# A two-layer decoder step on one core: the stores of the first FFN phase go to GpSimd, and the loads of the samples and of the residual are tied to their step

## The chip, the cores and the metric

The kernel runs on one core of a Trainium2 chip. The metric is the device time of one execution in microseconds (us); of several executions the median counts. A core has five engines that run side by side, each through its own list of instructions in order: TensorE (PE, matrix products, with its weight loads shown apart as PEld), VectorE (DVE), ScalarE (ACT), GpSimd (POOL) and SyncE (SP). Any of SP, ACT and GpSimd can issue a DMA; an engine that has to wait before it may issue one also holds up everything behind it in its list.

## The reference

Two decoder layers over 1024 prompt rows and 8 samples of 8 rows each (1088 rows, width 1024), in float32. The change touches the second half of a layer, the gated FFN with a causal convolution of width 3 (5632 channels in, 2816 after the gate):

```python
h = _rmsnorm(x, p['g_ffn']) * (1 + sc_f) + sh_f
hu = h @ p['w_ffn_in']
ext = jnp.concatenate([conv_prev.astype(hu.dtype), hu], axis=1)
conv = p['conv_b'] + sum(p['conv_w'][j] * ext[:, j:j + t] for j in range(CONV_W))
gate, up = jnp.split(conv, 2, axis=-1)
x = x + g_f * ((jax.nn.silu(gate) * up) @ p['w_ffn_out'])
return x, k, v, vg, ext[:, -(CONV_W - 1):]
```

For the prompt `conv_prev` is zero; each sample brings two rows of its own. The last two rows of `ext` are an output too.

## The kernel before

Every float32 product is made of three products of a high and a low part (high x high, high x low, low x high). ACT rounds a tile to its high part and DVE subtracts to get the low part (`split`, L181 and L182).

The first FFN phase computes `hu` in 22 blocks f of 128 gate and 128 up channels, from seven products each (L916). Behind a block, `conv(f, i)` stores the 64 sample columns of `hu` to a scratch tensor `hsd` (L936, 32 KB) and its last two prompt columns to the output (L937, 1 KB), and makes the convolution of the prompt columns on ACT and DVE. `gate(f)` multiplies the two halves on DVE (L950) and stores the gated product to the scratch tensor `pd[f]` (L951, 512 KB). A layer has 44 + 44 + 22 = 110 such stores, and SP issues them between the loads of the weights.

The second FFN phase multiplies by `w_ffn_out`. `down(g)` is a pass over 22 steps f for one third of the 1088 columns (t = g // 2: 384, 384 and 320 columns) and one half of the output rows (mh = g % 2), g = 0 to 5. A step makes 12 matmuls (L304, L305, L306 for four PSUM banks). It needs the weight `ro`, split to `oh` and `ol` (`half_unit`, L1058: three raw buffers, six of each split part), and in passes with mh = 0 the product `pr` loaded from `pd` and split to `ph` (`load_prod`, L1052: three raw buffers; 25 split ones, so the next pass uses them again). Tile names carry layer, f, then mh and t: `ro1_1710` is layer 1, f = 17, mh = 1, t = 0, and `pr1_130` is layer 1, f = 13, t = 0.

`samples()` is called in the text at g = 1, f = 10. It loads the samples' rows `hs` from `hsd` (L1068, 1408 KB) and their old rows `hal` (L1071), copies both into `ext` (L1075 on ACT, L1074 on GpSimd), saves the new last rows (L1077, L1079), makes the convolution with six large DVE operations (L1090, L1091, and L1093, L1094 twice; tiles `sa` and `sm`), SiLU on ACT (L1096), the gate on DVE (L1097), and 22 stores of `sa` into the sample columns of `pd` (L1099, 32 KB each), which only the passes g = 4 and 5 read. At f = 8 of each pass `hook` loads the four residual tiles `xb` that the end of the pass needs (L1129); there L293 adds the products to the residual and L1118 or L1120 stores it.

In what order an engine runs all this is not set by the text alone: a scheduler places each instruction in its engine's list, as early as its buffers, its data and its own reckoning of time allow, so a load can go far ahead of the place where it is written. `after(a, b)` (L88) keeps instruction a behind instruction b in that placing, without a wait on the chip. The kernel uses it elsewhere already.

Of the kernel before, what the change touches and what calls it, by code (L numbers as in the profile page):

```python
# [16 lines left out]
P = 128  # L17
D = 1024
KD = D // P
NP = 1024  # L20
NSEQ = 8
DT = 8
# [5 lines left out]
NF = DFF // P  # L28
# [19 lines left out]
def hybrid_decoder_kernel(  # L48
# [5 lines left out]
    nc = tc.nc  # L54
# [15 lines left out]
    def big(shape, dt, nm):  # L70
        q = "bb" if nm.startswith(late) else "ba"
        return pl[q].tile(shape, dt, tag="b", name=nm, bufs=9)
# [4 lines left out]
    def bank(tag, nm):  # L77
        return pl["ps"].tile([P, 512], F32, tag=tag, name=nm, bufs=4)
# [9 lines left out]
    def after(inst, prev):  # L88
        tc.add_manual_dep(
            inst.ins, prev.ins.name,  # L90
            mybir.DependencyInfo(mybir.DependencyClass.NoSync, mybir.DependencyReason.DATA),
            reason="issue order")
# [64 lines left out]
    def unit(l, u, eng=nc.vector):  # L157
        wp = pl["wp"]
        raw = wp.tile([P, 1024], F32, tag="raw", name=f"r{l}_{u}", bufs=NRAW)
        nc.sync.dma_start(out=raw, in_=w[l, u])  # L160
        wh = wp.tile([P, 1024], F32R, tag="wh", name=f"wh{l}_{u}", bufs=6)
        wl = wp.tile([P, 1024], F32R, tag="wl", name=f"wl{l}_{u}", bufs=6)
        nc.scalar.activation(out=wh, in_=raw, func=AF.Copy)  # L163
        eng.tensor_tensor(out=wl, in0=raw, in1=wh.bitcast(F32), op=ALU.subtract)  # L164
        return wh, wl
# [136 lines left out]
    def mm3(pt, lh, ll, rh, rl, first, last):  # L302

        r = nc.tensor.matmul(pt, lhsT=lh, rhs=rh, start=first, stop=False)  # L304
        nc.tensor.matmul(pt, lhsT=lh, rhs=rl, start=False, stop=False)  # L305
        nc.tensor.matmul(pt, lhsT=ll, rhs=rh, start=False, stop=last)  # L306
        return r
# [97 lines left out]
    xs = [big([P, T], F32, f"x0_{m}") for m in range(KD)]  # L405
# [106 lines left out]
    for l in range(DEPTH):  # L512
# [10 lines left out]
        for g in range(4):  # L523
            wh, wl = unit(l, U_ZU + g)
            pts = [bank(tags[g % 2], f"zu{l}_{g}{t}") for t in range(3)]
# [255 lines left out]
        xo = dp.tile([KD, P, T], F32, tag=f"xo{l}", name=f"xo{l}")  # L781
# [4 lines left out]
        xs = []  # L786
# [141 lines left out]
        pd = [dp.tile([P, T], F32, tag=f"pd{l}_{f}", name=f"pd{l}_{f}") for f in range(NF)]  # L928
        hsd = dp.tile([P, NCH, NS], F32, tag=f"hsd{l}", name=f"hsd{l}")
        hus, cvs, xps = {}, {}, {}  # L930

        def conv(f, i, to=bp):

            ch = i * NF + f
            hu = hus.pop((f, i))
            nc.sync.dma_start(out=hsd[:, ch], in_=hu[:, NP:])  # L936
            nc.sync.dma_start(out=o_cp[l, :, ch], in_=hu[:, NP - 2:NP])  # L937
            a = cvs[f, i] = to(f"cv{l}_{f}{i}")
            w0, w1, w2 = (L[:, L_CW + j * NCH + ch:L_CW + j * NCH + ch + 1] for j in range(3))
            cb = L[:, L_CB + ch:L_CB + ch + 1]  # L940
            nc.scalar.activation(out=a[:, :NP], in_=hu[:, :NP], func=AF.Identity, scale=w2, bias=cb)  # L941
            for sh, wt in ((1, w1), (2, w0)):
                nc.vector.scalar_tensor_tensor(out=a[:, sh:NP], in0=hu[:, :NP - sh], scalar=wt,  # L943
                                               in1=a[:, sh:NP], op0=ALU.mult, op1=ALU.add)
            if i == 0:
                nc.scalar.activation(out=a[:, :NP], in_=a[:, :NP], func=AF.Silu)  # L946

        def gate(f):
            g, u = cvs.pop((f, 0))[:, :NP], cvs.pop((f, 1))[:, :NP]
            nc.vector.tensor_tensor(out=u, in0=g, in1=u, op=ALU.mult)  # L950
            nc.sync.dma_start(out=pd[f][:, :NP], in_=u)  # L951

        def tail(f):
            prod(xps[f], "T4", "A22", False, True)
# [31 lines left out]
        for i in range(2):  # L986
            conv(0, i, lambda nm: first[1][:, i])
# [55 lines left out]
        xs = []  # L1043
        for m in range(KD):
            xs.append(pl["xb"].tile([P, T], F32, tag=f"x{m}", name=f"xb{l}m{m}", bufs=1))
        acc = {"of": lambda nm: pl["xb"].tile([P, T], F32, tag="acc", name=nm, bufs=1)}
        prods = {}

        def load_prod(f, t):
            o, n = THIRDS[t]  # L1050
# [13 lines left out]
        def samples():  # L1064

            sc = pl["sc"]
            hs = sc.tile([P, NCH * NSEQ, DT], F32, tag="hs", name=f"hs{l}", bufs=1)
            nc.sync.dma_start(out=hs, in_=hsd.rearrange("p c (s i) -> p (c s) i", i=DT))  # L1068
            hal = sc.tile([P, NCH * NSEQ, 2], F32, tag="hal", name=f"hal{l}", bufs=1)
            for i in range(2):  # L1070
                nc.sync.dma_start(out=hal[:, i * NF * NSEQ:(i + 1) * NF * NSEQ],  # L1071
                                  in_=halo[l, i].rearrange("p f s j -> p (f s) j"))
            ext = sc.tile([P, NCH * NSEQ, 2 + DT], F32, tag="ext", name=f"ext{l}", bufs=1)
            nc.gpsimd.tensor_copy(ext[:, :, :2], hal)  # L1074
            nc.scalar.activation(out=ext[:, :, 2:], in_=hs, func=AF.Copy)  # L1075
            new = sc.tile([P, NCH * NSEQ, 2], F32, tag="new", name=f"new{l}", bufs=1)
            nc.gpsimd.tensor_copy(new, ext[:, :, DT:])  # L1077
            for i in range(2):
                nc.sync.dma_start(out=o_cs[l, i].rearrange("p f s j -> p (f s) j"),  # L1079
                                  in_=new[:, i * NF * NSEQ:(i + 1) * NF * NSEQ])  # L1080
            a = sc.tile([P, NCH, NSEQ, DT], F32, tag="a", name=f"sa{l}", bufs=1)
            tm = sc.tile([P, NCH, NSEQ, DT], F32, tag="hs", name=f"sm{l}", bufs=1)

            def rows(j):
                return ext[:, :, j:j + DT].rearrange("p (c s) i -> p c s i", s=NSEQ)

            def per(o):
                return L[:, o:o + NCH].unsqueeze(2).unsqueeze(3).to_broadcast([P, NCH, NSEQ, DT])

            nc.vector.tensor_tensor(out=a, in0=rows(2), in1=per(L_CW + 2 * NCH), op=ALU.mult)  # L1090
            nc.vector.tensor_tensor(out=a, in0=a, in1=per(L_CB), op=ALU.add)  # L1091
            for j in (1, 0):
                nc.vector.tensor_tensor(out=tm, in0=rows(j), in1=per(L_CW + j * NCH), op=ALU.mult)  # L1093
                nc.vector.tensor_tensor(out=a, in0=a, in1=tm, op=ALU.add)  # L1094
            af = a.rearrange("p c s i -> p c (s i)")
            nc.scalar.activation(out=af[:, :NF], in_=af[:, :NF], func=AF.Silu)  # L1096
            nc.vector.tensor_tensor(out=af[:, NF:], in0=af[:, :NF], in1=af[:, NF:], op=ALU.mult)  # L1097
            for f in range(NF):
                nc.sync.dma_start(out=pd[f][:, NP:], in_=af[:, NF + f])  # L1099

        def down(g, hook):
            t, mh = divmod(g, 2)
            o, n = THIRDS[t]
            pts = [bank(tags[g % 2], f"y{l}_{g}{i}") for i in range(4)]
            for f in range(NF):
                wh, wl = half_unit(f, mh, t)
                if mh == 0:
                    load_prod(f, t)
                for i in range(4):
                    mm3(pts[i][:, :n], wh[:, i * P:(i + 1) * P], wl[:, i * P:(i + 1) * P], prods[f][:, 0, :n],  # L1110
                        prods[f][:, 1, :n], f == 0, f == NF - 1)
                hook(f)
            for i in range(4):
                m = 4 * mh + i
                residual(l, t, xs[m], pts[i], 5, m, f"y{l}{g}")
                if l + 1 < DEPTH:
                    square_sum(acc, xs[m], t, m, f"n{l}")
                    nc.sync.dma_start(out=xd[m, :, o:o + n], in_=xs[m][:, o:o + n])  # L1118
                else:
                    nc.sync.dma_start(out=y[m, :, o:o + n], in_=xs[m][:, o:o + n])  # L1120
# [4 lines left out]
        def hook(f):  # L1125
            if f == 8:
                o, n = THIRDS[g // 2]
                for m in range(4 * (g % 2), 4 * (g % 2) + 4):
                    nc.sync.dma_start(out=xs[m][:, o:o + n], in_=xo[m, :, o:o + n])  # L1129
            if g == 1 and f == 10:  # L1130
                samples()
            if l + 1 < DEPTH:
                if g in (2, 4):
                    if g == 2 and f == 0:
                        A1[0] = norm_scale(l + 1, L_GA, 1, f"a{l + 1}")
                    if f == 2:
                        hht, gen[0] = norm(l + 1, g // 2 - 1, xs, acc, A1[0], 0, f"a{l + 1}")
                        h.append(hht)
                    elif f > 2:
                        advance(gen[0], 1)  # L1140
                if g in (1, 3) and 1 <= f <= 8:
                    ada_tag[0] = "mm"
                    ada(1, 1)
                    ada_tag[0] = "at"
# [162 lines left out]
```

## Time and profile before

| | |
|---|---|
| median of 3 runs | 2339.3 us (2336.26 to 2341.22) |
| profiled execution | 2337.34 us, of which its span 2335.5 |
| TensorE's clock, mean | 0.988 of full speed |
| busy: PE, DVE, ACT, GpSimd | 2257.0, 1568.4, 1070.2, 93.6 us |

The span runs from the first to the last instruction of one profiled execution. Busy time does not count the issuing of DMAs. An engine that is idle off the chain of work that ends last costs nothing. TensorE's clock has two levels, 2.4 GHz (1.00 in the table by stretch) and 1.2 GHz (0.50); a stretch with both shows a value between them.

### The profile page before, as it was taken

Reading aid. Unit: us, or ns where it says so; the run is one execution under the profiler, and the core shown is the slowest. Engines: PE = TensorE matmul, PEld = TensorE weight load, DVE = VectorE, ACT = ScalarE, POOL = GpSimd, SP = SyncE. Lnnn points to the kernel's source line nnn. Section 1 sums busy time; section 2 is a strip of 40 time slices with the busy share of each in tenths; the row PEclk is TensorE's granted clock in tenths of the full one; section 3 lists DMA queues with packets and bytes.
Section 4 is the critical chain, followed back from the end, with each engine's and each line's share of the span. In section 5 each row is a group of like instructions: output and inputs, shape, how many; then the busy total and the mean of one; then the engine's idle time right before and its main releaser. Section 6 shows DMA issues by size and latency. Waiting matters only on the chain.

```text
span 2335.5 us, 40665 instructions
## 1 busy us (share of the span) xinstructions
PE 2257.0 (97%) x15838; PEld 2127.7 (91%) x15838; DVE 1568.4 (67%) x3238; ACT 1070.2 (46%) x2026; POOL 93.6 (4%) x78
## 2 busy tenths in 40 slices
PE   7999999999999998999999999989999999969999
PEld 5898789899999998899989977789999999969999
DVE  6837845987777777574667488269777777675543
ACT  5525534644444444354544355246444444444442
POOL 1000002000000000000100000110000000000000
PEclk9999999999999999999999999999999999989999
DMA  9220244322222226867441002741222222187653
GB/s 350 101 89 1 75 165 163 123 81 85 77 82 79 76 68 224 276 212 246 155 156 48 32 1 96 247 139 48 85 77 76 77 84 78 57 262 239 202 186 131
DMA packets 163489, 294.78 MB, mean 126 GB/s; under 512 B 47200, under 2 KB 88800, under 8 KB 163040
## 3 DMA queue, kind: packets, MB, share of 16 engines
q1 hardware_dynamic: 163296, 292.18, 37.5%
q8 instruction: 124, 2.03, 0.3%
q14 instruction: 69, 0.57, 0.1%
HBM read 245.42 MB, written 46.69 MB: 125 GB/s over the span
## 4 chain that ended last, share of the span: by engine, by line
PE 88%; DVE 4%; DMA 3%; ACT 2%; issue 1%; SPq 1%; POOL 0%; DVEq 0%; ACTq 0%; POOLq 0%
PE X L916 23%; PE Y L916 11%; PE o L313 7%; PE y L306 7%; PE y L304 7%; PE y L305 7%; PE Z L916 6%; PE zu L313 4%; PE s L644 2%; PE ada L130 1%; PE av L732 1%; PE q L304 1%; PE zv L306 1%; PE zv L305 1%; PE q L305 1%; PE zv L304 1%
## 5 line engine op out<-in xcount | busy, mean ns | idle before, releaser
L304 PE MATMUL y<-ph,oh 128*128 128x384 f32 (+1 forms) x1056 | 347.9, 331 | 24.2 <-ACT oh L181 18.6
L305 PE MATMUL y<-ph,oh 128*128 128x384 f32 (+1 forms) x1056 | 348.3, 330 | 2.8 <-DVE ph L182 2.8
L306 PE MATMUL y<-ph,ol 128*128 128x384 f32 (+1 forms) x1056 | 347.4, 329 | 0.9 <-DVE ol L182 0.9
L182 DVE TENSOR_TENSOR ol<-ro,oh 128x512 fp32r<-128x512 f32 x264 | 183.3, 702 | 188.5 <-ACT oh L181 177.1
L181 ACT ACTIVATE oh<-ro 128x512 fp32r<-128x512 f32 x264 | 165.8, 630 | 256.0 <-DMA ro<-in_w 123.8
L943 DVE SCALAR_TENSOR_TENSOR cv<-hu,lc,cv 128x1023 f32<-128x1023 f32 (+1 forms) x168 | 215.3, 1282 | 48.2 <-ACT cv L941 46.6
L304 PEld LDWEIGHTS y<-ph,oh 128*128 128x128 f32 x1056 | 200.1, 190 | 31.8 <-ACT oh L181 22.5
L305 PEld LDWEIGHTS y<-ph,oh 128*128 128x128 f32 x1056 | 201.0, 190 | 3.5 <-DVE ph L182 3.5
L306 PEld LDWEIGHTS y<-ph,ol 128*128 128x128 f32 x1056 | 200.8, 190 | 1.5 <-DVE ol L182 1.5
L313 PE MATMUL o<-hhm,wh 128*128 128x384 f32 (+1 forms) x384 | 120.8, 334 | 0.0
L313 PE MATMUL o<-hhm,wl 128*128 128x384 f32 (+1 forms) x384 | 119.1, 330 | 0.3 <-DVE wl L164 0.3
L313 PE MATMUL o<-hlm,wh 128*128 128x384 f32 (+1 forms) x384 | 118.8, 329 | 0.4 <-DVE hlm L182 0.4
L941 ACT ACTIVATE cv<-hu,lc 128x1024 f32<-128x1024 f32 x84 | 104.5, 1244 | 26.4 <-DVE hu L1006 25.0
L163 ACT ACTIVATE wh<-r 128x1024 fp32r<-128x1024 f32 x44 | 46.3, 1056 | 93.6 <-PE zu L313 64.8
L164 DVE TENSOR_TENSOR wl<-r,wh 128x1024 fp32r<-128x1024 f32 x40 | 48.9, 1224 | 54.4 <-ACT wh L163 44.7
L950 DVE TENSOR_TENSOR cv<-cv,cv 128x1024 f32<-128x1024 f32 x42 | 52.0, 1239 | 46.7 <-ACT cv L946 46.7
L181 ACT ACTIVATE ph<-pr 128x384 fp32r<-128x384 f32 (+1 forms) x132 | 64.2, 500 | 38.1 <-DMA pr<-pd 35.7
L182 DVE TENSOR_TENSOR ph<-pr,ph 128x384 fp32r<-128x384 f32 (+1 forms) x132 | 69.0, 546 | 16.4 <-ACT ph L181 16.4
L313 PEld LDWEIGHTS o<-hhm,wh 128*128 128x128 f32 x384 | 71.7, 189 | 6.6 <-issue 5.3
L313 PEld LDWEIGHTS o<-hhm,wl 128*128 128x128 f32 x384 | 71.8, 189 | 2.2 <-issue 1.6
L313 PEld LDWEIGHTS o<-hlm,wh 128*128 128x128 f32 x384 | 71.7, 189 | 2.0 <-DVE hlm L182 1.0
L916 PE MATMUL Z<-A12h,B21l 128*128 128x272 f32 x352 | 73.0, 289 | 0.0
(398 smaller groups left out, 6033.5 us busy)
## 6 DMA issues: line engine op xcount, KB each, us to landing
r<-in_w SPq DMA_DIRECT2D x132, 512.0 KB, 3.5
ro<-in_w SPq DMA_DIRECT2D x264, 256.0 KB, 3.2
ra<-in_w_ada SPq DMA_DIRECT2D x64, 512.0 KB, 4.5
pd<-cv SPq DMA_DIRECT2D x42, 512.0 KB, 2.6
pr<-pd SPq DMA_DIRECT2D x88, 192.0 KB, 3.8
rb<-in_w_ada SPq DMA_DIRECT2D x16, 512.0 KB, 8.3
ra<-in_w_ada SPq DMA_DIRECT2D x32, 256.0 KB, 4.1
pr<-pd SPq DMA_DIRECT2D x44, 160.0 KB, 3.4
```

The lines of the kernel that those rows point to most:

```text
L164: eng.tensor_tensor(out=wl, in0=raw, in1=wh.bitcast(F32), op=ALU.subtract)
L181: r = nc.scalar.activation(out=h, in_=x, func=AF.Copy)
L182: eng.tensor_tensor(out=lo, in0=x, in1=h.bitcast(F32), op=ALU.subtract)
L304: r = nc.tensor.matmul(pt, lhsT=lh, rhs=rh, start=first, stop=False)
L305: nc.tensor.matmul(pt, lhsT=lh, rhs=rl, start=False, stop=False)
L306: nc.tensor.matmul(pt, lhsT=ll, rhs=rh, start=False, stop=last)
L313: nc.tensor.matmul(pts[t][:, :n], lhsT=lhsT, rhs=r[t][:, k, :], start=f, stop=e)
L644: nc.tensor.matmul(pss[g][:, 256 * (c % 2):256 * (c % 2) + 256], lhsT=qt[:, a, q], rhs=kz[:, g, b].rearrange("p b j -> p (b j)"), start=f, ...
L916: nc.tensor.matmul(pt[:, i, :HC], lhsT=a[:, k * P:(k + 1) * P], rhs=b[:, k, i * HC:(i + 1) * HC], start=(first and k == 0 and a is wh and ...
L941: nc.scalar.activation(out=a[:, :NP], in_=hu[:, :NP], func=AF.Identity, scale=w2, bias=cb)
L943: nc.vector.scalar_tensor_tensor(out=a[:, sh:NP], in0=hu[:, :NP - sh], scalar=wt, in1=a[:, sh:NP], op0=ALU.mult, op1=ALU.add)
L950: nc.vector.tensor_tensor(out=u, in0=g, in1=u, op=ALU.mult)
```

## The change

The stores of the first FFN phase, L936, L937 and L951, are issued by GpSimd instead of SP. `down` notes its last product in `mark[0]`, and the loads of `hs` and `hal` and of the residual tiles are placed behind the product noted when their call is reached: for the samples that of g = 1, f = 10, for the residual that of f = 8 of the pass.

```diff
-            nc.sync.dma_start(out=hsd[:, ch], in_=hu[:, NP:])
-            nc.sync.dma_start(out=o_cp[l, :, ch], in_=hu[:, NP - 2:NP])
+            nc.gpsimd.dma_start(out=hsd[:, ch], in_=hu[:, NP:])
+            nc.gpsimd.dma_start(out=o_cp[l, :, ch], in_=hu[:, NP - 2:NP])
...
-            nc.sync.dma_start(out=pd[f][:, :NP], in_=u)
+            nc.gpsimd.dma_start(out=pd[f][:, :NP], in_=u)
...
-        prods = {}
+        prods, mark = {}, [None]
...
-            nc.sync.dma_start(out=hs, in_=hsd.rearrange("p c (s i) -> p (c s) i", i=DT))
+            after(nc.sync.dma_start(out=hs, in_=hsd.rearrange("p c (s i) -> p (c s) i", i=DT)), mark[0])
...
-                nc.sync.dma_start(out=hal[:, i * NF * NSEQ:(i + 1) * NF * NSEQ],
-                                  in_=halo[l, i].rearrange("p f s j -> p (f s) j"))
+                after(nc.sync.dma_start(out=hal[:, i * NF * NSEQ:(i + 1) * NF * NSEQ],
+                                        in_=halo[l, i].rearrange("p f s j -> p (f s) j")), mark[0])
...
-                    mm3(pts[i][:, :n], wh[:, i * P:(i + 1) * P], wl[:, i * P:(i + 1) * P], prods[f][:, 0, :n],
-                        prods[f][:, 1, :n], f == 0, f == NF - 1)
+                    mark[0] = mm3(pts[i][:, :n], wh[:, i * P:(i + 1) * P], wl[:, i * P:(i + 1) * P],
+                                  prods[f][:, 0, :n], prods[f][:, 1, :n], f == 0, f == NF - 1)
...
-                    nc.sync.dma_start(out=xs[m][:, o:o + n], in_=xo[m, :, o:o + n])
+                    after(nc.sync.dma_start(out=xs[m][:, o:o + n], in_=xo[m, :, o:o + n]), mark[0])
```

The first place is the seam between the two phases, in layer 1. SP's list before, from the last sample store of phase 1 to the first weight of g0:

```order
L936 DMA hsd1_17185<-hu1_210_22311 128x64
L937 DMA out_cp<-hu1_210_22311 128x2
L1052 DMA pr1_20_22582<-pd1_2_17165 128x384
L1071 DMA hal1_23256<-in_halo 128x352 x2
L1052 DMA pr1_30_22605<-pd1_3_17166 128x384
L1068 DMA hs1_23254<-hsd1_17185 128x2816
L951 DMA pd1_21_17184<-cv1_211_22457 128x1024
L1052 DMA pr1_40_22628<-pd1_4_17167 128x384
L1052 DMA pr1_50_22651<-pd1_5_17168 128x384
L1052 DMA pr1_60_22674<-pd1_6_17169 128x384
L1058 DMA ro1_000_22530<-in_w 128x512
```

And now:

```order
L1052 DMA pr1_20_22582<-pd1_2_17165 128x384
L1052 DMA pr1_30_22605<-pd1_3_17166 128x384
L1052 DMA pr1_40_22628<-pd1_4_17167 128x384
L1052 DMA pr1_50_22651<-pd1_5_17168 128x384
L1052 DMA pr1_60_22674<-pd1_6_17169 128x384
L1052 DMA pr1_70_22697<-pd1_7_17170 128x384
L1052 DMA pr1_80_22720<-pd1_8_17171 128x384
L1058 DMA ro1_000_22530<-in_w 128x512
```

The three stores, `hal` and `hs` are gone from here, and the products 7 and 8, which stood behind the first weights, stand ahead of them. ACT's list at the same place, before:

```order
L946 ACTIVATE cv1_210_22488<-cv1_210_22488 128x1024
L181 ACTIVATE ph1_30_22607<-pr1_30_22605 128x384
L1075 ACTIVATE ext1_23259<-hs1_23254 128x352x8
L181 ACTIVATE ph1_40_22630<-pr1_40_22628 128x384
L181 ACTIVATE ph1_50_22653<-pr1_50_22651 128x384
L181 ACTIVATE ph1_60_22676<-pr1_60_22674 128x384
L181 ACTIVATE oh1_000_22532<-ro1_000_22530 128x512
```

And now:

```order
L946 ACTIVATE cv1_210_22488<-cv1_210_22488 128x1024
L181 ACTIVATE ph1_30_22607<-pr1_30_22605 128x384
L181 ACTIVATE ph1_40_22630<-pr1_40_22628 128x384
L181 ACTIVATE ph1_50_22653<-pr1_50_22651 128x384
L181 ACTIVATE ph1_60_22676<-pr1_60_22674 128x384
L181 ACTIVATE ph1_70_22699<-pr1_70_22697 128x384
L181 ACTIVATE ph1_80_22722<-pr1_80_22720 128x384
L181 ACTIVATE oh1_000_22532<-ro1_000_22530 128x512
```

The copy `ext`, which waits for `hs`, is gone from the seam. The seam of layer 0 changes in the same way. The second place is DVE's list where the samples' operations stand. Before, in g0 (layer 1), one of the six behind every six splits:

```order
L1090 TENSOR_TENSOR sa1_23266<-ext1_23259,lc1_1322 128x2816
L182 TENSOR_TENSOR ol1_000_22533<-ro1_000_22530,oh1_000_22532 128x512
L182 TENSOR_TENSOR ol1_100_22556<-ro1_100_22553,oh1_100_22555 128x512
L182 TENSOR_TENSOR ol1_200_22579<-ro1_200_22576,oh1_200_22578 128x512
L182 TENSOR_TENSOR ph1_40_22630<-pr1_40_22628,ph1_40_22630 128x384
L182 TENSOR_TENSOR ph1_50_22653<-pr1_50_22651,ph1_50_22653 128x384
L182 TENSOR_TENSOR ph1_60_22676<-pr1_60_22674,ph1_60_22676 128x384
L1091 TENSOR_TENSOR sa1_23266<-sa1_23266,lc1_1322 128x2816
```

Now, at the end of g1 (steps 17 to 21, then step 0 of g2):

```order
L182 TENSOR_TENSOR ol1_1710_23409<-ro1_1710_23406,oh1_1710_23408 128x512
L1090 TENSOR_TENSOR sa1_23266<-ext1_23259,lc1_1322 128x2816
L1093 TENSOR_TENSOR sm1_23267<-ext1_23259,lc1_1322 128x2816
L1091 TENSOR_TENSOR sa1_23266<-sa1_23266,lc1_1322 128x2816
L182 TENSOR_TENSOR ol1_1810_23427<-ro1_1810_23424,oh1_1810_23426 128x512
L1094 TENSOR_TENSOR sa1_23266<-sa1_23266,sm1_23267 128x2816
L182 TENSOR_TENSOR ol1_1910_23445<-ro1_1910_23442,oh1_1910_23444 128x512
L1093 TENSOR_TENSOR sm1_23267<-ext1_23259,lc1_1322 128x2816
L182 TENSOR_TENSOR ol1_2010_23463<-ro1_2010_23460,oh1_2010_23462 128x512
L1094 TENSOR_TENSOR sa1_23266<-sa1_23266,sm1_23267 128x2816
L182 TENSOR_TENSOR ol1_2110_23481<-ro1_2110_23478,oh1_2110_23480 128x512
L182 TENSOR_TENSOR ol1_001_23515<-ro1_001_23512,oh1_001_23514 128x512
```

Behind them come one residual operation (L293), L1097, three more L293 and then `ol1_101`, the weight of step 1. ACT's copy `ext` stands between the weights 17 and 18 of g1, and `hs` on SP behind the load of weight 17. The third place is SP's list around the 22 stores of `sa`. Before, they lay in g1 of layer 1 in groups of three between the weights, and the last twelve in a row (in layer 0, 21 in a row). Now, at the start of g2:

```order
L1058 DMA ro1_301_23581<-in_w 128x512
L1120 DMA out_y<-xb1m4_22522 128x384
L1099 DMA pd1_0_17163<-sa1_23266 128x64
...
L1099 DMA pd1_21_17184<-sa1_23266 128x64
L1120 DMA out_y<-xb1m5_22523 128x384
L1120 DMA out_y<-xb1m6_22524 128x384
L1120 DMA out_y<-xb1m7_22525 128x384
L1058 DMA ro1_401_23604<-in_w 128x512
```

All 22 stand in one block between the weights of steps 3 and 4 of g2, with the residual's stores around them; the lists of layer 0 have the block at the same place.

## Rows read from the trace of the kernel before

**Rows 1.** The page: busy time of the engines, and the DMA queue.

```profile
PE 2257.0 (97%) x15838; PEld 2127.7 (91%) x15838; DVE 1568.4 (67%) x3238; ACT 1070.2 (46%) x2026; POOL 93.6 (4%) x78
...
q1 hardware_dynamic: 163296, 292.18, 37.5%
```

**Rows 2.** By stretch: length; PE, PEld, DVE, ACT, POOL busy; PE clock, DMA share, GB/s.

```profile
429.11:895.68 466.57, 466.57 (x3722) 466.35 (x3721) 352.62 (x448) 228.23 (x328) 0.00 (x0) 1.00 0.24 78
895.68:954.49 58.81, 50.42 (x265) 49.49 (x266) 49.60 (x56) 29.80 (x47) 4.68 (x2) 0.91 0.86 281
2048.67:2116.37 67.70, 49.16 (x265) 48.65 (x266) 53.15 (x62) 33.98 (x56) 4.55 (x2) 0.85 0.84 272
2116.37:2162.30 45.93, 45.93 (x266) 45.93 (x266) 25.11 (x43) 21.16 (x39) 0.00 (x0) 1.00 0.76 239
```

**Rows 3.** PE's waits, 895 to 915.5 and 2048 to 2117: total, times, longest.

```profile
PE y L304 <- ACT ph L181: 5.5, 2, 2.8
PE y L305 <- DVE ph L182: 2.8, 1, 2.8
...
PE y L304 <- ACT oh L181: 17.6, 1, 17.6
PE y L306 <- DVE ol L182: 0.9, 1, 0.9
```

**Rows 4.** ACT's timeline at the seam of layer 1: start, duration, what.

```profile
2061.88 2.58 ACT L1075 ACTIVATE ext<-hs 128x2816 f32<-128x2816 f32 x1 [6.52 <-DMA hs<-hsd]
...
2065.60 1.74 ACT L181 ACTIVATE oh<-ro 128x512 fp32r<-128x512 f32 x3
```

**Rows 5.** DVE's timeline at the seam of layer 0.

```profile
911.20 3.09 DVE L1090 TENSOR_TENSOR sa<-ext,lc 128x2816 f32<-128x2816 f32 x1 [3.15 <-ACT ext L1075]
```

**Rows 6.** SP's waits, 429.11 to 895.68.

```profile
SPq L936 <- ACT hu L955: 160.0, 20, 8.3
```

**Rows 7.** SP's timeline at the seam of layer 1.

```profile
2056.34 0.32 SPq L951 DMA_DIRECT2D pd<-cv  x1
...
2059.12 1.82 SPq L1058 DMA_DIRECT2D ro<-in_w  x3
```

**Rows 8.** By stretch, as rows 2: stretches behind waits, with a lower clock.

```profile
915.44:919.90 4.46, 4.46 (x14) 4.46 (x15) 4.46 (x5) 1.46 (x3) 0.00 (x0) 0.50 0.68 209
2066.26:2073.61 7.35, 6.40 (x19) 5.89 (x20) 7.35 (x8) 2.34 (x4) 2.00 (x1) 0.50 0.52 158
1017.78:1022.30 4.52, 4.52 (x21) 4.52 (x22) 3.50 (x9) 1.04 (x2) 0.00 (x0) 0.62 0.71 210
```

**Rows 9.** The page's DMA issues: count, KB each, median us to landing.

```profile
ro<-in_w SPq DMA_DIRECT2D x264, 256.0 KB, 3.2
```

**Rows 10.** By tile, `hs` (landing), then `sa`: duration in ns, min/median/max.

```profile
DMA to landing us min/median/max: 8.8/8.9/9.1
...
L1094 DVE TENSOR_TENSOR sa<-sa,sm x4: 3079/3081/3082, 930.1 to 2098.0; 128x2816 f32<-128x2816 f32 x4
...
L1099 SPq DMA_DIRECT2D pd<-sa x44: 319/430/443, 952.7 to 2131.3; - x44
```

**Rows 11.** DVE's timeline in layer 1, end of the samples' work and end of g0.

```profile
2104.20 1.62 DVE L1097 TENSOR_TENSOR sa<-sa 128x1408 f32<-128x1408 f32 x1
...
2117.31 2.19 DVE L293 SCALAR_TENSOR_TENSOR xb1m<-y,mod,xb1m 128x384 f32<-128x384 f32 x4
2119.41 0.68 DVE L182 TENSOR_TENSOR ol<-ro,oh 128x512 fp32r<-128x512 f32 x1
```

**Rows 12.** SP's timeline in g1 of layer 0.

```profile
971.63 9.94 SPq L1099 DMA_DIRECT2D pd<-sa  x21
```

**Rows 13.** PE's waits, 954 to 1030.

```profile
PE nrma L216 <- POOL accn L206: 3.3, 1, 3.3
PE nrba L239 <- DVE dga L238: 1.1, 1, 1.1
PE y L304 <- ACT oh L181: 1.1, 1, 1.1
```

## The prediction

> **What bounds the kernel now.** I read the page's totals first: TensorE (PE) is busy 97% of the span [rows 1], so only an edit that moves PE's idle time, or its clock, can move the time. Where that idle time is stands in the table by stretch [rows 2]. The first FFN phase has none: PE is busy 466.57 of 466.57 us in layer 0, and layer 1 reads the same. In the second phase six passes of 22 steps follow, which I call g0 to g5. A pass without a stall is the 45.93 us of layer 1's g1, so a step costs 45.93 / 22 = 2.09 us. Against that, the way from the last product of phase 1 to the end of g0 takes 58.81 us in layer 0 and 67.70 us in layer 1: 12.9 and 21.8 us lost.
>
> Second, PE's waits by their releaser [rows 3]. Layer 0 waits twice for ACT's split of a product (5.5 us in all) and once for DVE's (2.8 us); layer 1 waits 17.6 us for ACT's first weight split and 0.9 us for DVE. Third, the timelines at those places. In layer 1 [rows 4] ACT is done with the 4th product at 2055.4, stands 6.52 us for the samples' rows `hs`, copies them (`ext`, 2.58 us), splits three products and only at 2065.60 the first weight. In layer 0 the same copy, and then DVE's first sample operation of 3.09 us [rows 5], stand ahead of product 4.
>
> **The change part by part.**
> *The stores.* 220 DMAs leave SP's sequence. Where they stood SP waited (160.0 us for ACT alone, in layer 0 [rows 6]), but with PE's idle time at zero there [rows 2] this gives nothing inside phase 1: the weight loads' lead hides it. Only at the seam to phase 2 does SP's order bear on PE: in layer 1 the store of the last gated product, for which SP waits until 2056.34 (DVE's gate), stands ahead of products 4 to 6 and of weight 0, issued at 2059.12 [rows 7].
>
> *Seam of layer 0.* The new order has no `ext`, no sample operation and no `hs` before g1. The second wait for ACT and the one for DVE go, 2.7 + 2.8 = 5.5 us (the first wait, for product 0, stays), and with them the stretch of 4.46 us at clock 0.50 behind them [rows 8], half of it lost: 2.2 us. Gain 7.7.
>
> *Seam of layer 1.* Nothing holds ACT at `ext` any more. Products have three raw buffers, so product 6 still waits for DVE's split of product 3, which stands behind the gate. The new order puts nine products ahead of weight 0, so three of them (6 to 8 in place of 4 to 6) still lie between the gate and weight 0; only the store's own slot of 0.4 us goes: weight 0 issued at 2058.8, landed 3.2 us later [rows 9], split in 0.6: PE starts at 2062.6 instead of 2066.26, gain 3.6. The 0.9 us wait for DVE, behind the sample operation, goes. The cold stretch of 7.35 us [rows 8] I leave, since PE has still been idle for 14 us. Gain 4.5. Bounds: 2 (the weight lands in 6 us) and 8 (the cold loss of 7.35 less 0.9, halved, 3.2 us, goes too). Both seams: 12.2 us, from 9.7 to 15.7.
>
> *Where the samples' work goes: the end of g1.* Here the order decides. Let G be the start of g1. Six buffers of split weights mean that weight k is split when step k-6 is through; a raw buffer (three) comes free with its DVE split. So weight 17 is loaded when weight 14 is split: G + 9 x 2.09 + 1.3 = G+20.1, and `hs` behind it at about G+21. It lands after 8.9 us [rows 10]: G+29.9, `ext` until G+32.5. DVE then has, before weight 21 is through, six sample operations of 3.08 us [rows 10] and four splits of 0.68 us [rows 11], which overlap by some hundredths each: 20.5 us, to G+53. PE needs weight 21's low part 0.7 us before the end of the pass, so g1 ends at about G+53.5 instead of G+45.9: **7.5 us** a layer. Before, the same operations lay in g0, one behind every six splits, and were over at 2105.8 [rows 11]; g1 ran unstalled behind them. The least it can be: `hs` in the 3.2 us of a weight of a fifth of its size [rows 9]; then `ext` waits for its turn behind weight 17's split, which needs step 11 done, G+25.7: 4.2 us earlier, 3.3 left.
>
> *Behind it, DVE.* The split of weight 1 of g2 stands behind L1097 (1.62 us) and four residual operations (2.19 us) [rows 11]. PE has weight 0 and works 2.09 us on it: **2.1 us**, bounds 1 and 2.4.
>
> *Behind that, SP.* The 22 stores of the samples' products now form one block between weights 3 and 4 of g2. They wait for L1097, which ends about D+2.3, D being the start of g2. In a row a store costs 9.94 / 21 = 0.47 us of SP's time [rows 12], so the block is out at D+12.7; three residual stores behind it, at the same price, D+14.1; weight 4 lands at D+17.3 and is split at D+18. PE wants it at D + 4 x 2.09 + 2.1 = D+10.5: **7.5 us**. The nearest row is layer 0's block of 21 in g1, before which PE had all six weights in stock: it lost 1.1 us [rows 12, 13]. Now it has four, and the block starts 2.3 us after PE has begun on them, so I take the worked value; at the store's minimum of 0.32 us [rows 10] the block takes 7.0 us and the stall is 4.1; at most 9.
>
> *Clock.* Behind a wait of 2.8 us the clock was 0.50 for 4.46 us, behind one of 3.3 us it was 0.62 for 4.52 us [rows 8]: losses of 2.2 and 1.7 us. For the two long stalls of a layer I take **2.5 us** together, bounds 1.7 and 3.4.
>
> *Residual loads.* 24 DMAs a layer go to step 8 of their own pass. They leave g0, where the DMA share is 0.84 to 0.86 [rows 2], and have 13 steps, 27 us, until they are used, against a few us of landing: nothing. If they were late, each would cost its landing, about 3 us, once.
>
> *Sum.* A layer loses 7.5 + 2.1 + 7.5 + 2.5 = 19.6 us. Layer 0 lost part of that already at these places: waits of 3.3, 1.1 and 1.1 us [rows 13] and 1.7 us of clock, 7.2, all of them before step 4 of g2 and so covered by the longer stalls; that leaves 12.4. Loss 32.0, gain 12.2: +19.8. The profiled execution took 2337.3 (span 2335.5 and 1.8 around it): 2357. Bounds: a layer from 3.3 + 1 + 4.1 + 1.7 = 10.1 to 8.5 + 2.4 + 9 + 3.4 = 23.3, where 8.5 is the first stall with `hs` 1 us later; so 20.2 - 7.2 - 15.7 = -2.7 to 46.6 - 7.2 - 9.7 = +29.7, or 2335 to 2367. The median of the runs shown is 2.0 us above the profiled one, well inside the range.
>
> **The rivals.**
> *Faster.* The samples' work is hidden in g1. For it: DVE is busy only 25.11 of 45.93 us in g1 [rows 2], and 6 x 3.08 = 18.5 us would fit. Against it: the new order packs them into its last 13 us. It decides if `ext` is done 7.5 us earlier than I reckon, by G+25, and if SP is out of its block before PE has used its four weights, which D+12.7 against D+8.4 speaks against. Then only the gains remain: 2337.3 - 12.2 = 2325.
>
> *No difference.* The stalls are half what I reckon (the lower bounds above), or GpSimd's stores and the ties move nothing that counts: about 2340. Within 0.2%, about what a measurement of this kernel can tell from no change, means 4.7 us either way.
>
> *Phase 1 becomes slower.* GpSimd issues no DMA before: the page has one queue beside those that load instructions [rows 1], and GpSimd is busy 0.00 us in phase 1 [rows 2]. If its stores hold up DVE, or must wait until DVE is idle and keep a buffer so long, all that is to be had is DVE's 466.57 - 352.62 = 114 us of idle time [rows 2], and 110 stores have to live on it: 1.04 us each. At 2 us, the price is 110 x 0.96 = 106 us a layer, 2550. No row shows such a store; SP's waits of 160 us in a phase without any wait of PE show how late a store may be there, and that speaks against it. On this the Trainium skill, SBUF — State Buffer, section "SBUF: two separate sides", warns of a trap: while DVE runs certain fast operations, GpSimd cannot write the descriptors of its DMAs, and the remedy is to issue them from SP or ACT, the reverse of this change. No run so far shows it here.
>
> **How the numbers follow.** The forecast (both stalls, in each layer, their price open): 0.66, of which 0.04 lies within 0.2% of before. No difference: 0.13, of which 0.02 ends just beyond that on the slow side. Faster: 0.15. Phase 1 slower: 0.06. So faster 0.15, same 0.15, slower 0.70. The range leaves out the faster rival and phase 1, 0.21 in all, and reaches over the bounds of the sum: 2335 to 2367.
>
> **What would show it.** Right: no waits around product 4 in layer 0; layer 1's g0 begins some 14 us after its phase 1 instead of 17.6; PE waits for DVE's `ol` in steps 18 to 21 of g1, behind `sa` and `sm`; then 2 us at step 1 and some 7 us at step 4 of g2 for ACT's weight split, with SP full of `pd<-sa` until then, in both layers; g1 and g2 of layer 1 together near 110 us instead of 91.9. Wrong: `hs` issued well before G+21, the block of stores hidden, or idle time of PE in phase 1.

## The result: 25 us slower, and where they are in the profile

The changed kernel takes 2364.32 us (2364.04 to 2364.43, 4 runs) against 2338.81 us before: a ratio of 1.0109, 95% interval 1.0092 to 1.0127. That is 25.5 us more, inside the range and 7 us above the predicted time. The profiled execution took 2364.26 us (span 2362.1), 26.6 us of span more than before.

The page of the changed kernel, engines and DMA queues (to be read beside [rows 1]):

```profile
PE 2266.5 (96%) x15838; PEld 2135.6 (90%) x15838; DVE 1568.7 (66%) x3238; ACT 1068.5 (45%) x2026; POOL 212.6 (9%) x298
...
q0 software_dynamic: 11968, 26.06, 3.0%
```

GpSimd has become busier by 119 us and has a DMA queue of its own kind. Unlike SP's, its issuing of a DMA is counted as busy time here: 220 issues of 0.54 us are these 119 us. Of the others PE has changed most, by 9.5 us (its weight loads by 7.9) for the same 15838 matmuls. The table by stretch (length; PE, PEld, DVE, ACT, POOL busy; PE clock, DMA share, GB/s) has, in order, phase 1 of both layers, the seam with g0 of both layers, and g1 and g2 of layer 1:

```profile
430.66:899.01 468.35, 468.35 (x3722) 467.92 (x3721) 352.70 (x448) 227.98 (x328) 57.88 (x107) 1.00 0.23 78
1588.24:2054.86 466.62, 466.62 (x3722) 466.41 (x3721) 347.33 (x439) 224.18 (x321) 57.82 (x107) 1.00 0.22 74
899.01:949.45 50.44, 47.65 (x266) 47.42 (x266) 32.82 (x52) 27.24 (x49) 1.62 (x3) 0.97 0.79 248
2054.86:2119.33 64.47, 48.80 (x266) 48.56 (x266) 37.19 (x59) 31.61 (x56) 1.62 (x3) 0.87 0.68 216
2119.33:2174.54 55.21, 48.56 (x265) 47.92 (x265) 36.52 (x38) 20.20 (x35) 4.64 (x2) 0.94 0.58 188
2174.54:2234.18 59.64, 48.84 (x265) 47.97 (x265) 27.90 (x45) 20.69 (x35) 0.00 (x0) 0.91 0.61 191
```

PE has no idle time in phase 1, as before. The seam (the way from the end of phase 1 to PE's first product of g0) together with g0 has become shorter by 8.4 us in layer 0 (58.81 before, [rows 2]) and by 3.2 in layer 1 (67.70). Then the loss: g1 and g2 of layer 1 take 55.21 + 59.64 = 114.85 us where an unstalled pass takes 45.93 [rows 2], 23 us more. PE's waits say the same of both layers (waits in 950 to 1071, layer 0, then 2054 to 2235, layer 1; total, times, longest):

```profile
PE y L304 <- ACT oh L181: 7.3, 2, 7.0
PE y L306 <- DVE ol L182: 6.8, 2, 4.9
PE nrba L239 <- DVE dga L238: 0.6, 1, 0.6
...
PE y L304 <- ACT oh L181: 25.7, 3, 15.7
PE y L306 <- DVE ol L182: 7.4, 2, 5.6
```

The 15.7 us are the seam of layer 1 (17.6 before, [rows 3]); the rest is new, but for the 5.5 us of [rows 13], in whose place the layer 0 waits stand. What DVE was at when PE waited for `ol` in layer 1, and then SP when PE waited for `oh`:

```profile
2153.36 3.09 DVE L1090 TENSOR_TENSOR sa<-ext,lc 128x2816 f32<-128x2816 f32 x1 [5.27 <-ACT ext L1075]
2156.37 3.74 DVE L1093 TENSOR_TENSOR sm<-ext,lc 128x2816 f32<-128x2816 f32 x1
2160.03 3.08 DVE L1091 TENSOR_TENSOR sa<-sa,lc 128x2816 f32<-128x2816 f32 x1
2163.03 0.68 DVE L182 TENSOR_TENSOR ol<-ro,oh 128x512 fp32r<-128x512 f32 x1
...
2173.84 1.28 DVE L182 TENSOR_TENSOR ol<-ro,oh 128x512 fp32r<-128x512 f32 x2
```
```profile
2141.80 0.38 SPq L1068 DMA_DIRECT2D hs<-hsd  x1
...
2177.62 10.29 SPq L1099 DMA_DIRECT2D pd<-sa  x22
2188.01 1.33 SPq L1120 DMA_DIRECT2D out_y<-xb1m  x3
2189.44 1.38 SPq L1058 DMA_DIRECT2D ro<-in_w  x3
```

From 2153.4 to 2174.5 DVE gets four weights of g1 done in 21 us, where PE uses one in 2.09 us. The 22 stores then hold SP for 10.29 us, and weight 4 of g2 goes out at 2189.4, 15 us after g2 began.

### The profile page after: what moved, and what is told of

Read it like the earlier page. It is cut to its first block, busy times and chain, and to the rows that moved or that the text cites. A ratio compares the mean times of both kernels' runs of the same rounds, so it can differ in the third digit from the quotient of the medians.

```text
span 2362.1 us, 40791 instructions
## 1 busy us (share of the span) xinstructions
PE 2266.5 (96%) x15838; PEld 2135.6 (90%) x15838; DVE 1568.7 (66%) x3238; ACT 1068.5 (45%) x2026; POOL 212.6 (9%) x298
## 4 chain that ended last, share of the span: by engine, by line
PE 88%; DVE 5%; DMA 3%; ACT 2%; issue 1%; SPq 1%; POOL 0%; DVEq 0%; ACTq 0%; POOLq 0%
PE X L916 22%; PE Y L916 11%; PE o L313 7%; PE y L304 7%; PE y L306 6%; PE y L305 6%; PE Z L916 6%; PE zu L313 4%; PE s L644 2%; PE zv L306 1%; PE zv L305 1%; PE av L732 1%; PE zv L304 1%; PE ada L130 1%; PE q L304 1%
## 5 line engine op out<-in xcount | busy, mean ns | idle before, releaser
L306 PE MATMUL y<-ph,ol 128*128 128x384 f32 (+1 forms) x1056 | 344.8, 333 | 14.4 <-DVE ol L182 14.2
L306 PEld LDWEIGHTS y<-ph,ol 128*128 128x128 f32 x1056 | 202.1, 192 | 17.1 <-DVE ol L182 17.1
L936 POOL DMA_DIRECT2D hsd<-hu x84 | 45.4, 540 | 523.4 <-ACT hu L955 448.8
```

## The experiments

Each was timed beside the kernel before on the same chip; ratios are to that.

**Which part carries the loss.** First the stores alone:

```diff
-            nc.sync.dma_start(out=hsd[:, ch], in_=hu[:, NP:])
-            nc.sync.dma_start(out=o_cp[l, :, ch], in_=hu[:, NP - 2:NP])
+            nc.gpsimd.dma_start(out=hsd[:, ch], in_=hu[:, NP:])
+            nc.gpsimd.dma_start(out=o_cp[l, :, ch], in_=hu[:, NP - 2:NP])
...
-            nc.sync.dma_start(out=pd[f][:, :NP], in_=u)
+            nc.gpsimd.dma_start(out=pd[f][:, :NP], in_=u)
```

> Only the three stores of phase 1 are issued by GpSimd; no load is tied. The order puts the samples' rows and operations back to the seam and into g0, spread as before. Theory (the loss lies at the end of g1 and the start of g2, the stores cost nothing): no difference, 2334 to 2343 us, phase 1 at 466.6 us in both layers, the waits at both seams as in the kernel before. Rival (stores issued by GpSimd carry a part of the 25 us): 2346 or more, with PE idle in phase 1 or products landing late at the seam.

2336.45 us against 2338.67, ratio 0.9989 (0.9980 to 0.9998). They cost nothing; the seam's wait in layer 1 is 14.2 us instead of 17.6, where the small gain of 0.1% would fit.

Then the ties alone, of the samples and of the residual, with the stores left on SP (the other hunks of the change):

> Only the ties of both kinds of loads; the stores of phase 1 stay with SP. The order has the same chain of sample operations at the end of g1 and the same block of 22 stores in g2. Theory: the whole loss is here, 2358 to 2368 us, with the same four gaps of PE in g1 and g2. Rival (the stores carry it): 2339.

2363.35 us, 1.0106 (1.0091 to 1.0121): the whole loss. Its waits in layer 1 are those of the changed kernel. Its phase 1 in layer 0 takes 468.09 us, with GpSimd busy for 0.00, so the 468.35 us of the changed kernel (466.57 before) aren't the stores' doing:

```profile
431.47:899.56 468.09, 468.09 (x3722) 467.88 (x3721) 353.14 (x448) 228.09 (x328) 0.00 (x0) 1.00 0.24 78
```

They lie in its first microseconds, which ran at a lower clock: the first 4 us of phase 1 of layer 0 in the changed kernel, in the one with the ties alone, and before:

```profile
430.66:434.66 4.00, 4.00 (x22) 4.00 (x22) 3.71 (x8) 3.78 (x7) 0.00 (x0) 0.57 0.00 0
431.47:435.47 4.00, 4.00 (x22) 4.00 (x22) 3.71 (x8) 3.77 (x7) 0.00 (x0) 0.58 0.00 0
429.11:433.11 4.00, 4.00 (x34) 4.00 (x34) 3.72 (x8) 3.78 (x7) 0.00 (x0) 1.00 0.00 0
```

Of the two ties, now that of the residual alone (with the stores on GpSimd): the changed kernel with `after` taken off the loads of `hs` and `hal`:

```diff
-            after(nc.sync.dma_start(out=hs, in_=hsd.rearrange("p c (s i) -> p (c s) i", i=DT)), mark[0])
+            nc.sync.dma_start(out=hs, in_=hsd.rearrange("p c (s i) -> p (c s) i", i=DT))
```

> Stores of phase 1 by GpSimd and the residual loads tied, the samples' loads free as before: the order has them at the seam again. Theory (the residual ties alone cost and bring little): 2332 to 2339 us, g0 of both layers with the waits for the samples' copy as before. Rival (the residual ties carry part of the loss): 2345 or more.

2339.52 us, 0.9999 (0.9990 to 1.0008): no difference; the median is half a microsecond above the expected span of values. So the loss comes with the samples' tie; that tie without the residual's was not run in this place.

**Taking the two suspected waits apart.** The changed kernel with the 22 stores of a layer off SP:

```diff
-                nc.sync.dma_start(out=pd[f][:, NP:], in_=af[:, NF + f])
+                nc.gpsimd.dma_start(out=pd[f][:, NP:], in_=af[:, NF + f])
```

> The changed kernel, with the 22 stores of the samples' products a layer issued by GpSimd too, so that no block stands on SP ahead of weight 4 of g2. Theory (that block is the releaser of the wait at step 4): the gaps of 9.0 us in layer 1 and 7.0 us in layer 0 go, with about 1.5 us of slow clock each; in layer 0 the norm's wait of some 3 us that was covered comes back: 2346 to 2350 us. Rival (weight 4 is late because raw buffers came free late behind DVE's chain): the gap at step 4 stays, above 2358.

2350.51 us, 1.0044 (1.0029 to 1.0059), half a microsecond above the expected span of values. PE's waits in layer 1, 2054 to 2222:

```profile
PE y L304 <- ACT oh L181: 16.0, 3, 15.5
PE y L306 <- DVE ol L182: 6.8, 2, 4.9
```

The wait of 9.0 us at step 4 of g2 is gone, and with it 14 us of time; the waits for `ol` stay. That block of stores was its releaser, and the rival, raw buffers that come free late, is out. Now the other one: the stores stay on SP, and DVE's chain is made shorter. This kernel leaves out two of the three taps of the samples' convolution, so its outputs for the samples differ.

```diff
-            for j in (1, 0):
-                nc.vector.tensor_tensor(out=tm, in0=rows(j), in1=per(L_CW + j * NCH), op=ALU.mult)
-                nc.vector.tensor_tensor(out=a, in0=a, in1=tm, op=ALU.add)
```

> The changed kernel, with four of the six large sample operations on DVE left out (the samples' convolution keeps one tap of three, so their output differs). The block of 22 stores stays on SP, now behind weight 2 of g2. Theory (PE's waits for the low parts of weights 18 to 21 are the length of DVE's chain, 6 operations of 3.08 us): with 12.3 us less in the chain these waits, 5.6 and 4.9 us, are gone or under 0.5 us, and with them the wait of 1.1 us for weight 21; the gap at the block stays at 7 to 11 us. 2349 to 2357 us. Rival (the waits come from the samples' rows landing late, or from raw buffers): they stay above 3 us.

2342.48 us, 1.0012 (1.0003 to 1.0021). PE's waits in layer 1, 2043 to 2211:

```profile
PE y L304 <- ACT oh L181: 22.7, 2, 15.9
PE y L306 <- DVE ol L182: 1.0, 1, 1.0
```

With 12.3 us out of the chain, the wait for the low parts of weights 18 to 21 is gone; 1.0 us is left, in g1, and the wait at the block is 6.7 us in layer 1 and 3.0 in layer 0. The releaser is DVE's chain. The total came out 6.5 us under the lower end of what was expected: I had put the block at no less than 7 us in both layers, which is 4.3 us of it; the rest I haven't placed.

**Is it the later place, or the chain?** The text of the samples' work stays at g = 1, f = 10, but its loads are placed behind step 2 of g0:

```diff
-        prods, mark = {}, [None]
+        prods, mark, early = {}, [None], [None]
...
-            after(nc.sync.dma_start(out=hs, in_=hsd.rearrange("p c (s i) -> p (c s) i", i=DT)), mark[0])
+            after(nc.sync.dma_start(out=hs, in_=hsd.rearrange("p c (s i) -> p (c s) i", i=DT)), early[0])
...
+            if g == 0 and f == 2:
+                early[0] = mark[0]
```

> The changed kernel with the samples' loads tied to step 2 of g0 in place of step 10 of g1, the text of the samples' work left where it is. The order spreads the six DVE operations over g0 and g1 with several weight splits between, and puts the 22 stores behind weight 10 of g1. Theory (what costs is the samples' operations in one chain between weight splits, not that they run later): the gains at the seams stay (8.4 and 3.2 us), the stalls in g1 and g2 go but for about 1 us a layer at the block of stores, as in layer 0 before: 2327 to 2332 us. Rival (the loss is the loads' late place itself, or DVE has no room for them): above 2345.

2349.22 us, 1.0042 (1.0027 to 1.0056): my total missed by 17 us or more and lies where the rival had put it. PE's waits decide between the two. The part on DVE was right: PE waits for no `ol` in layer 1 any more, so DVE does have room for the samples' work here. What I had taken for 1 us, the block of stores in g1 with all six weights ahead, is 11.1 us there (waits in 2049 to 2220, then SP's timeline):

```profile
PE y L304 <- ACT oh L181: 27.3, 2, 16.2
```
```profile
2129.19 9.80 SPq L1099 DMA_DIRECT2D pd<-sa  x19
2139.04 1.85 SPq L1129 DMA_DIRECT2D xb1m<-xo  x4
2140.93 1.38 SPq L1099 DMA_DIRECT2D pd<-sa  x3
2142.41 1.33 SPq L1058 DMA_DIRECT2D ro<-in_w  x3
```

The block has drawn the four residual loads into it and holds SP for 13.2 us; by the time it starts, PE is in step 7 of g1 with weights up to step 10 loaded, so part of the six is used. In layer 0 it costs 4.7 us, where the conditioning's matmuls make g1's steps longer. So a block before which the stock looks full isn't cheap. Nor was it full in layer 0 before, as the prediction took it to be: that block began at 971.63, when PE was in step 6 with weights up to step 10 loaded. Its 1.1 us [rows 13] had two things in its favour: layer 0's slower pass (g1 took 53.72 us there before, 45.93 in layer 1), and a block of 9.94 us [rows 12] without the residual's loads in it. Which of them counts for how much these runs don't separate.

Both together, the early tie and the 22 stores by GpSimd:

> The samples' loads tied to step 2 of g0, as in the run before, and the 22 stores of the samples' products issued by GpSimd. Theory (of the two parts of the loss, the chain on DVE and the block on SP, both are gone now): the gaps of 11.1 us in g1 of layer 1 and 4.7 us in layer 0 go, with some 3 us of slow clock each at most: 2326 to 2331 us, faster than the kernel before by the gains at the seams. Rival (stores from GpSimd, or the samples' operations wherever they stand, still cost): above 2337.

2334.17 us (2328.0 to 2336.92), 0.9972 (0.9960 to 0.9983): a little faster than the kernel before, and clearly than the changed one. The profiled execution is its fastest, 2328.0, so the rows below are those of a fast execution; the median is 3 us above what I expected, and what spreads its six runs over 9 us I don't know. PE's waits in layer 1, 2040 to 2200, and DVE's list, in which the sample operations now have splits between them:

```profile
PE y L304 <- ACT oh L181: 16.1, 1, 16.1
PE y L306 <- DVE ol L182: 0.2, 1, 0.2
```
```profile
2101.31 3.08 DVE L1094 TENSOR_TENSOR sa<-sa,sm 128x2816 f32<-128x2816 f32 x1
2104.32 0.69 DVE L182 TENSOR_TENSOR ol<-ro,oh 128x512 fp32r<-128x512 f32 x1
2105.80 0.69 DVE L182 TENSOR_TENSOR ol<-ro,oh 128x512 fp32r<-128x512 f32 x1 [0.80 <-ACT oh L181]
2106.41 3.08 DVE L1093 TENSOR_TENSOR sm<-ext,lc 128x2816 f32<-128x2816 f32 x1
```

In layer 1 only the seam is left. With `f == 5` for `f == 2`:

> As the first run of this set, the samples' loads tied to step 5 of g0 instead of step 2. Layer 1's order hardly differs. Layer 0's puts the rows behind product 12 instead of 9. Theory: the same to within 2 us, 2325 to 2331 us. Rival (where in g0 they stand matters, since g0 loads products and weights): more than 3 us apart.

2332.55 us, 0.9964 (0.9952 to 0.9977): 1.6 us apart, intervals over each other; the place within g0 isn't what matters, though the median is 1.6 us above what I expected.

**What else belongs to the faster version.** With the stores of phase 1 back on SP:

> The faster version (samples' loads tied to step 2 of g0, the 22 sample stores by GpSimd, residual loads tied), with the stores of phase 1 back on SP. Theory (those stores bring no more than the two to three microseconds that the run with them alone showed, all of it at the seam): 2333 to 2339 us, at most 3 us behind the faster version, phase 1 without a wait of PE. Rival (the seam gains hang on the stores being off SP): as the kernel before, 2338 or more, with a seam of 17 us or more in layer 1.

2330.84 us, 0.9971 (0.9960 to 0.9982), no different. Neither version has a stall that hangs on where these stores are issued; in layer 1 the seam's wait is 14.8 us, the rival's 17 is out, and the time is 2 us under the span of values that I had given.

With the residual loads untied (`after` taken off L1129):

> The faster version with the residual loads not tied. The order then lets them run into g0 and moves the samples' work itself to the end of g0 and the first half of g1. Theory (the residual ties cost nothing and bring a microsecond or two by keeping 4.6 MB out of g0): 2332 to 2340 us. Rival (they are worth nothing): the same as the faster version, 2330 to 2334.

2341.39 us, 1.0006 (0.9997 to 1.0014). By the ratios this is some 8 us behind the faster version, and outside both expectations. In its order the loads that run ahead push the samples' rows back (in layer 1 the copy `ext` starts at 2099.6, in a g0 that began at 2064.9 and ended at 2116.9); behind the seam its waits in g0 to g2 of layer 1 are 4.0 us instead of 0.2, and those in g1 of layer 0 6.5 us instead of 0.4. What of it is the residual's transfers and what the samples' later place this run doesn't separate.

## Why the prediction was right, step by step

- **Stores in phase 1, zero:** right. In phase 1 GpSimd took 0.54 us for an issue, SP had taken 0.32 to 0.42, and `pd` landed in 2.9 us instead of 2.6; PE did not wait for it. The rival on phase 1 is out by the stores-alone run. The Trainium skill, SBUF — State Buffer, "SBUF: two separate sides", describes the trap named beside that rival. No run here shows it: DVE was busy for 352.70 of 468.35 us beside these stores, and PE waited for none of them; that DVE ran any of the operations that the page means is not shown either.
- **Seam of layer 0, gain 7.7:** 8.4 measured; both waits and the slow stretch behind them are gone.
- **Seam of layer 1, gain 4.5:** 3.2 measured. PE starts 15.7 us after phase 1, not 14. The step that failed is the landing of weight 0, taken as 3.2 us, the median of all weights. It went out 10.0 us after phase 1, as reckoned, but ACT could start on it only 5.0 us later. ACT split products 7 and 8 just before, which came late as well, but then still stood 0.16 us for the weight. At this place a weight had taken 6.2 us before, too, so the 3.2 us was the wrong row to take. Before, DMAs issued from 2052 to 2069; then, now, SP's and ACT's timeline:

```profile
ro<-in_w SPq DMA_DIRECT2D x4, 256.0 KB, 6.2
...
2064.85 1.65 SPq L1058 DMA_DIRECT2D ro<-in_w  x3
...
2068.71 0.99 ACT L181 ACTIVATE ph<-pr 128x384 fp32r<-128x384 f32 x2 [2.73 <-DMA pr<-pd]
2069.86 1.30 ACT L181 ACTIVATE oh<-ro 128x512 fp32r<-128x512 f32 x2 [0.16 <-DMA ro<-in_w]
```

- **DVE's chain, 7.5 a layer:** 5.6 + 1.05 us of waits in layer 1 and 4.9 in layer 0. `hs` went out at G+22.5 instead of G+21 (in layer 1) and landed after 8.9 us, as taken. The 5.6 us are one wait, for the low part of weight 18, over at 2163.76; in steps 19 to 21, where the prediction saw such waits too, there is none. PE then ran at clock 0.50 until 2168.64 (under "Clock"): 15 matmuls in 4.88 us are, as an estimate, 3.9 us for a step of 12, while DVE gave a weight every 3.6 us. So part of what the chain costs is in the clock's term. The 1.05 us is a second effect, not reckoned: a raw buffer comes free only when its weight's split gets its turn in the chain, so the loads behind weight 20 go out late. By the order of the lists the weight that PE waits for is weight 0 of g2, split at 2170.79 (weight 21, named in the expectation of the run with the taps left out, was split before it):

```profile
2166.51 0.63 ACT L181 ACTIVATE oh<-ro 128x512 fp32r<-128x512 f32 x1 [10.38 <-DMA ro<-in_w]
2170.79 0.63 ACT L181 ACTIVATE oh<-ro 128x512 fp32r<-128x512 f32 x1 [3.65 <-DMA ro<-in_w]
```

  That the chain is the cause is shown by the run with the taps left out.
- **Weight 1 of g2, 2.1:** 1.8 and 1.9.
- **The block of stores, 7.5:** 9.0 in layer 1, 7.0 in layer 0 (with 0.6 at the norm), the price of a store in a row 10.29 / 22 = 0.47 as taken. Shown by the run with these stores on GpSimd.
- **Clock, 2.5 a layer:** the term that was mis-sized. g1 and g2 of layer 1 are 23.0 us longer than 2 x 45.93, of which waits are 5.6 + 1.05 + 1.8 + 9.0 = 17.5; 5.5 us are clock: PE's busy time is longer by that much. Two waits of that length each have a slow stretch of their own behind or around them (by stretch, as above):

```profile
2161.81:2168.64 6.83, 4.88 (x15) 4.88 (x16) 6.83 (x5) 0.63 (x1) 0.00 (x0) 0.50 0.15 45
2189.12:2199.36 10.24, 5.40 (x17) 5.17 (x18) 4.14 (x7) 4.06 (x8) 0.00 (x0) 0.50 0.87 276
```

  PE's 4.88 and 5.40 us of work there would be half as long at full clock: 2.4 + 2.7 us. I had taken the loss once for the two.
- **The sum, +19.8:** in span -8.4 - 3.2 + 13.3 (g1 and g2 of layer 0) + 23.0 + 1.9 (all the rest) = 26.6. Of the 6.8 us over the sum, 3.4 are in layer 1's two passes, nearly all of it clock, 0.9 in layer 0's, 0.6 at the seams, and 1.9 in the rest of the kernel. Of these, 1.8 us are phase 1 of layer 0, with the slow clock at its start that the kernel with the ties alone shows too; why the clock is lower there than before is open. The misses of the single waits partly cancel: the chain's was 0.9 us too long, the block's 1.5 us too short.

The rival on the fast side failed at the place that was given for it: DVE has the room, but not in one chain. With the chain spread and the block gone, the rival's gain, 12 us, came out as 6 to 8. The rival of no difference, with the stalls at half, is out: the waits in g1 and g2 of layer 1 come to 17.5 us, where the prediction's three stalls were put at 17.1.

## What to carry to other kernels

Tying a load to a later step ties all that hangs on it: when it lands, its consumers are ready at once, and here they were placed ahead of the regular supply of the main loop, six large operations with single splits between them instead of one every six splits. Tie the load only as far as the seam needs, and leave its consumers the whole time until their result is wanted. A block of small stores on the queue that feeds the main loop costs its length, and the landing and split of the first load behind it, less the stock that is left when the block starts; here another engine issued it at no cost that showed.

## What was not expected of the hardware

DVE's L1093 took 3.73 and 3.74 us in the changed kernel, where the same operation takes 3.08 us elsewhere. A GpSimd copy (L1077) overlaps it by 0.8 us in both layers. First, from layer 1 of the changed kernel, the copies on GpSimd and three splits on DVE with no copy beside them; then the same operations before, on GpSimd and DVE:

```profile
2151.75 0.87 POOL L1074 COPY ext<-hal 128x704 f32<-128x704 f32 x1 [88.62 <-DMA hal<-in_halo]
2153.39 3.77 POOL L1077 COPY new<-ext 128x704 f32<-128x704 f32 x1 [0.77 <-ACT ext L1075]
...
2179.09 1.89 DVE L182 TENSOR_TENSOR ol<-ro,oh 128x512 fp32r<-128x512 f32 x3
```
```profile
2064.52 3.74 POOL L1077 COPY new<-ext 128x704 f32<-128x704 f32 x1 [9.27 <-ACT ext L1075]
...
2064.49 3.09 DVE L1090 TENSOR_TENSOR sa<-ext,lc 128x2816 f32<-128x2816 f32 x1 [7.71 <-ACT ext L1075]
2067.50 2.50 DVE L182 TENSOR_TENSOR ol<-ro,oh 128x512 fp32r<-128x512 f32 x3
```

The copy is the one that stands out: L1074 moves as much in 0.87 us. In all twelve traces and both layers L1077 starts just behind L1090 (2153.39 against 2153.36) and ends 0.65 to 0.71 us after it, and the operation that DVE runs next is longer by some 0.65 us, whatever it is: in the changed kernel L1093, before the first of three splits (the three take 2.50 us instead of 1.89). So the rows read as if the two took turns: the copy waits for L1090, and DVE's next operation for the copy. No run took the copy away from that place, so this stays a reading. It made the chain 0.65 us longer, but not only in the changed kernel: before, a split paid it.
